# The last store of a row sum, issued by two engines in two halves of the partitions

## The chip, the cores and the metric

The kernel runs on one core of a Trainium2 chip. A core has several engines with queues of their own; three matter here. VectorE (DVE) reduces and adds, ScalarE (ACT) applies a function and can sum what it reads, and SyncE (SP) issues transfers. ScalarE can issue transfers as well. All transfers, whoever issues them, are moved by 16 DMA engines. The metric is the time of one execution on the device in microseconds; lower is better.

## The reference

The input x has 32 x 512 x 1024 values in 32-bit floating point, 67 MB. The output is the sum of each row of 1024 values, so 16,384 sums, 64 KB.

```python
def reference(x):
    return np.sum(x, axis=-1).astype(np.float32)
```

## The kernel before

The 16,384 rows are laid over 128 partitions, so each partition has J = 128 rows. They come in blocks of 16 rows for each partition (BIG), 8 blocks in all. The first 16 x 128 rows of x are one region (x_a, out_a in the code) and the others a second (x_b, out_b, with TWO = 112 rows for each partition). Within a region a partition's rows, and so its sums in the output, lie side by side. The sums are gathered in one tile, sums, of 128 partitions by 128 columns; column j is row j of each partition.

SP issues all loads, in the order in which they are written (helper load, line 93). The first load brings 7 rows of the last block; then come the seven whole blocks, through three buffers, each load waiting until VectorE has summed the block whose buffer it takes. The other 9 rows of the last block come at the end in smaller loads: six rows, two rows, and the last row in two pieces of 536 and 488 values ("left" and "right").

VectorE sums the whole blocks with one instruction each (helper vec, line 100). The rows of the last block are shared out: helper halves (line 109) lets VectorE sum one row by adding its two halves, helper act (line 129) lets ScalarE sum one row. The last row is VectorE's: the left piece first, and then the right piece together with the left one's sum. Semaphores count what is done: acts for ScalarE's rows (10 of them), paired for VectorE's share of each piece (4 with the last row).

The output leaves in three stores. When ScalarE has 7 of its rows done and VectorE the first piece, and the two-row load has landed, ScalarE issues two early stores (lines 185 and 186): columns 16 to 111 to out_b, then columns 0 to 15 to out_a. It then waits for both to land (line 187, semaphore early). SP issues the last store (line 199), of the 16 columns of the last block, after it has waited for all four counts of paired and all of acts (lines 197 and 198), and then waits until it has landed (line 200, semaphore stored). Each of the three stores covers 128 partitions; the last writes 64 bytes for each partition, 8 KB together. Nothing comes after it in the program.

The order on each engine is as written; no planner moves instructions.

Of the kernel before, what the change touches and what calls it, by code (L numbers as in the profile page):

```python
# [30 lines left out]
def kernel(  # L31
# [5 lines left out]
    nc = tc.nc  # L37
# [8 lines left out]
    P = 128  # L46
    batch, seq, dim = x.shape
    rows = batch * seq
    J = rows // P
    BIG = 16  # L50
# [3 lines left out]
    TWO = J - ONE  # L54

    def region(first, n):
        lo, hi = first * P, (first + n) * P
        return (
            x_r[lo:hi, :].rearrange("(p j) d -> p j d", j=n),
            out_r[lo:hi].rearrange("(p j) -> p j", j=n),  # L60
        )

    x_a, out_a = region(0, ONE)
    x_b, out_b = region(ONE, TWO)
# [15 lines left out]
    sums = ctx.enter_context(nc.sbuf_tensor("sums", [P, J], fp32))  # L80
# [4 lines left out]
    def semaphore(name):  # L85
        return ctx.enter_context(nc.semaphore(name=name))

    def block_of(t, a, n):
        return t[:, a * dim : (a + n) * dim].rearrange("p (n d) -> p n d", d=dim)
# [17 lines left out]
    def halves(dst, src):  # L107
        n = src.shape[-1] // 2
        return nc.vector.tensor_tensor_reduce(  # L109
            out=src[:, :n],  # L110
            in0=src[:, :n],
            in1=src[:, n:],
            scale=1.0,
            scalar=0.0,
            op0=mybir.AluOpType.add,
            op1=mybir.AluOpType.add,
            accum_out=dst,
        )

    acts = semaphore("acts")  # L120
    n_acts = 0
# [34 lines left out]
    for landed, j, block in loads[:-1]:  # L156
# [11 lines left out]
    paired = semaphore("paired")  # L168
    pieces = (loads[-1] + (7,), (six, tail + FIRST, block_of(t, FIRST, 6), 2),
              (two, tail + FIRST + 6, block_of(t, FIRST + 6, 2), 1))  # L170
# [10 lines left out]
    early = semaphore("early")  # L181
# [2 lines left out]
    nc.scalar.wait_ge(two, 16)  # L184
    nc.scalar.dma_start(out=out_b[:, : TWO - BIG], in_=sums[:, ONE : J - BIG]).then_inc(early, 16)
    nc.scalar.dma_start(out=out_a, in_=sums[:, :ONE]).then_inc(early, 16)
    nc.scalar.wait_ge(early, 32)

    carried = semaphore("carried")
    nc.vector.wait_ge(left, 16)  # L190
# [2 lines left out]
    nc.vector.wait_ge(carried, 1)  # L193
    halves(sums[:, j : j + 1], whole).then_inc(paired, 1)

    stored = semaphore("stored")
    nc.sync.wait_ge(paired, len(pieces) + 1)
    nc.sync.wait_ge(acts, n_acts)
    nc.sync.dma_start(out=out_b[:, TWO - BIG :], in_=sums[:, J - BIG :]).then_inc(stored, 16)
    nc.sync.wait_ge(stored, 16)  # L200


# [28 lines left out]
```

## Time and profile before

| what | value |
|---|---|
| time, median of 3 runs | 160.7 us (160.56 to 160.77) |
| time of the profiled execution | 160.59 us |
| its span | 159.3 us |
| VectorE busy | 120.7 us, 76% |
| ScalarE busy | 11.9 us, 7% |
| HBM traffic over the span | 422 GB/s |
| chain that ended last | DMA 71%, DVE 27%, SP's queue 1% |

The span is what the hardware profiler records from the first to the last instruction; the time of the execution has 1.3 us more around it. Lines named L199 and the like are lines of the kernel file. A record of a DMA instruction (DMA_DIRECT2D) on SPq or ACTq is the time in which the engine's queue issues the transfer; the transfer itself comes after it and is seen in the busy share of the DMA engines. Waits on semaphores do not count as busy, and have a view of their own.

### The profile page before, as it was taken

How to read it: one execution, taken by the hardware profiler on the slowest of the kernel's cores; microseconds unless marked ns; L12 is line 12 of the kernel's file. 1: busy time of each engine (PE TensorE's matmuls, PEld its weight loads, DVE VectorE, ACT ScalarE, POOL GpSimd, SP SyncE). 2: the span in 40 equal slices, each digit the busy share in tenths (PEclk: the TensorE clock that was granted, in tenths of full speed). 3: DMA queues.
4: the chain of work that ended last, by engine and by line, in shares of the span. 5: the costliest groups of instructions: out<-in, count | busy, mean ns of one | idle time of the engine just before them, and what ended most of it. 6: DMA issues, size and time to landing. Idle time of an engine off the chain costs nothing.

```text
span 159.3 us, 122 instructions
## 1 busy us (share of the span) xinstructions
DVE 120.7 (76%) x40; ACT 11.9 (7%) x21; POOL 0.2 (0%) x4
## 2 busy tenths in 40 slices
DVE  0029600499985999779996899949999499994955
ACT  3000000000000000000000000000000000002993
POOL 0000000000000000000000000000000000000000
DMA  9899799699699699699698996996996996994984
GB/s 331 360 494 527 329 461 527 263 527 527 263 527 527 263 527 527 263 527 510 280 527 346 444 527 263 527 527 263 527 527 263 527 527 263 527 510 214 494 363 148
DMA packets 2160, 67.18 MB, mean 422 GB/s; under 512 B 624, under 2 KB 752, under 8 KB 880
## 3 DMA queue, kind: packets, MB, share of 16 engines
q1 hardware_dynamic: 1872, 67.12, 98.0%
q10 hardware_dynamic: 288, 0.06, 0.2%
HBM read 67.11 MB, written 0.07 MB: 422 GB/s over the span
## 4 chain that ended last, share of the span: by engine, by line
DMA 71%; DVE 27%; SPq 1%; issue 0%
DMA rows<-in_x_dram 71%; DVE sums L100 26%; SPq L93 1%; DVE rows L109 0%; DVE sums L109 0%
## 5 line engine op out<-in xcount | busy, mean ns | idle before, releaser
L100 DVE TENSOR_REDUCE sums<-rows 128x16 f32<-128x16384 f32 (+1 forms) x7 | 110.9, 15848 | 31.6 <-DMA rows<-in_x_dram 31.6
L129 ACT ACTIVATE unread<-rows 128x1024 f32<-128x1024 f32 x10 | 10.1, 1012 | 143.8 <-DMA rows<-in_x_dram 143.8
L109 DVE CUSTOM_DVE_ANT_0 rows<-rows 128x512 f32<-128x512 f32 (+2 forms) x16 | 9.6, 656 | 4.0 <-DMA rows<-in_x_dram 4.0
L129 ACT ACTIVATION_READ_ACCUMULATOR unread<-rows 128x1 f32 x10 | 1.9, 187 | 0.0
L129 ACT ACT_TABLE_LOAD x1 | 1.3, 1283 | 1.4 <-PEq L43 1.4
L109 DVE DVE_READ_ACCUMULATOR2_ANT sums<- 128x1 f32 x15 | 1.2, 83 | 0.0
L155 DVE MEMSET rows<- 128x1 f32 x1 | 0.1, 59 | 1.5 <-PEq L43 1.5
L215 POOL MEMSET const-bfloat16-1.0<- 128x1 bf16 x1 | 0.1, 102 | 0.0
L215 POOL MEMSET const-uint8-127<- 128x1 uint8 x1 | 0.1, 101 | 0.0
L215 POOL MEMSET const-float32-0.0<- 128x1 f32 x1 | 0.1, 99 | 0.2 <-issue 0.2
L215 POOL MEMSET const-float32-1.0<- 128x1 f32 x1 | 0.1, 98 | 0.0
L109 DVE DVE_READ_ACCUMULATOR2_ANT rows<- 128x1 f32 x1 | 0.1, 81 | 0.0
## 6 DMA issues: line engine op xcount, KB each, us to landing
rows<-in_x_dram SPq DMA_DIRECT2D x1, 3584.0 KB, 10.8
rows<-in_x_dram SPq DMA_DIRECT2D x1, 3072.0 KB, 28.7
rows<-in_x_dram SPq DMA_DIRECT2D x1, 1024.0 KB, 30.9
rows<-in_x_dram SPq DMA_DIRECT2D x1, 268.0 KB, 31.1
rows<-in_x_dram SPq DMA_DIRECT2D x1, 244.0 KB, 31.3
rows<-in_x_dram SPq DMA_DIRECT2D x7, 40.8
out_dram<-sums ACTq DMA_DIRECT2D x1, 48.0 KB, 1.6
out_dram<-sums ACTq DMA_DIRECT2D x1, 8.0 KB, 1.6
```

The source lines that it names most:

```text
L93: nc.sync.dma_start(out=dst, in_=src).then_inc(sem, 16)
L100: return nc.vector.tensor_reduce(out=sums[:, j : j + n], in_=block, axis=mybir.AxisListType.X, op=mybir.AluOpType.add,)
L109: return nc.vector.tensor_tensor_reduce(out=src[:, :n], in0=src[:, :n], in1=src[:, n:], scale=1.0, scalar=0.0, op0=mybir.AluOpType.add, op ...
L129: nc.scalar.activation(out=unread[n_acts % len(unread)][:, :], in_=src, func=mybir.ActivationFunctionType.Copy, accum_out=sums[:, j : j + ...
L155: nc.vector.memset(whole[:, width + 1 :], 0.0)
L215: nc = _bacc.Bacc("TRN2", target_bir_lowering=False, num_devices=1)
```

## The change

The last store is cut in two by partitions. SP stores the sums of partitions 0 to 63 and ScalarE those of partitions 64 to 127, 4 KB each. Both engines wait for the same counts of paired and acts first, and both stores count on the semaphore stored, so that SP's last wait is for 32 in place of 16. ScalarE's wait for its two early stores moves from directly behind them to behind its half of the last store.

```diff
     nc.scalar.dma_start(out=out_b[:, : TWO - BIG], in_=sums[:, ONE : J - BIG]).then_inc(early, 16)
     nc.scalar.dma_start(out=out_a, in_=sums[:, :ONE]).then_inc(early, 16)
-    nc.scalar.wait_ge(early, 32)
...
     stored = semaphore("stored")
-    nc.sync.wait_ge(paired, len(pieces) + 1)
-    nc.sync.wait_ge(acts, n_acts)
-    nc.sync.dma_start(out=out_b[:, TWO - BIG :], in_=sums[:, J - BIG :]).then_inc(stored, 16)
-    nc.sync.wait_ge(stored, 16)
+    half = P // 2
+    for engine, lo in ((nc.sync, 0), (nc.scalar, half)):
+        engine.wait_ge(paired, len(pieces) + 1)
+        engine.wait_ge(acts, n_acts)
+        engine.dma_start(
+            out=out_b[lo : lo + half, TWO - BIG :], in_=sums[lo : lo + half, J - BIG :]
+        ).then_inc(stored, 16)
+    nc.scalar.wait_ge(early, 32)
+    nc.sync.wait_ge(stored, 32)
```

## The prediction

> **What bounds the kernel now.** I read the chain of work that ended last first. 71% of it is the transfer of x, 26% VectorE's long reductions, and its last pieces are the row pieces in the closing microseconds. So the 67 MB of loads set the time until 157.35 us, and only what follows the last load can be touched by an edit of the last store. Next come the instructions in order of time from 156 us to the end.
>
> ```profile
> 156.13 0.37 ACTq L185 DMA_DIRECT2D out_dram<-sums  x1
> 156.53 0.56 ACTq L186 DMA_DIRECT2D out_dram<-sums  x1
> ...
> 157.01 0.19 ACT L129 ACTIVATION_READ_ACCUMULATOR unread<-rows 128x1 f32 x1
> ...
> 157.38 0.42 DVE L109 CUSTOM_DVE_ANT_0 rows<-rows 128x245 f32<-128x245 f32 x1 [0.17 <-DMA rows<-in_x_dram]
> 157.72 0.08 DVE L109 DVE_READ_ACCUMULATOR2_ANT sums<- 128x1 f32 x1
> 157.83 0.35 SPq L199 DMA_DIRECT2D out_dram<-sums  x1
> ```
>
> The reader sees start and duration. VectorE writes the last sum at 157.72 + 0.08 = 157.80; SP begins to issue the last store at 157.83 and is through with the issue at 158.18. ScalarE ended its last sum at 157.20 and its two early stores were issued by 157.09, so in the old kernel ScalarE's queue stands idle when the last sum is ready. What the issue costs in nanoseconds is in the answer on the output tensor, and what SP waits for after it in the waits of SP's queue (microseconds in all, times, longest):
>
> ```profile
> L185 ACTq DMA_DIRECT2D out_dram<-sums x1: 374/374/374, 156.1 to 156.1; - x1
> L186 ACTq DMA_DIRECT2D out_dram<-sums x1: 560/560/560, 156.5 to 156.5; - x1
> L199 SPq DMA_DIRECT2D out_dram<-sums x1: 348/348/348, 157.8 to 157.8; - x1
> ...
> SPq L200 <- DMA out_dram<-sums: 1.1, 1, 1.1
> ```
>
> 157.83 + 0.35 + 1.1 = 159.28, the end of the span (159.3). So the last store is 1.45 us on the path, 0.35 in the issue and 1.1 behind it. Where those 1.1 go is shown by stretches of 0.1 us; the last two columns are the busy share of the 16 DMA engines and GB/s:
>
> ```profile
> 157.50:157.60 0.10, 0.10 (x1) 0.00 (x0) 0.00 (x0) 1.00 0.01 1
> 157.60:157.70 0.10, 0.10 (x1) 0.00 (x0) 0.00 (x0) 1.00 0.47 53
> 157.70:157.80 0.10, 0.10 (x2) 0.00 (x0) 0.00 (x0) 1.00 0.27 29
> ...
> 158.50:158.60 0.10, 0.00 (x0) 0.00 (x0) 0.00 (x0) 1.00 0.00 0
> 158.60:158.70 0.10, 0.00 (x0) 0.00 (x0) 0.00 (x0) 1.00 0.12 13
> 158.70:158.80 0.10, 0.00 (x0) 0.00 (x0) 0.00 (x0) 1.00 0.62 55
> 158.80:158.90 0.10, 0.00 (x0) 0.00 (x0) 0.00 (x0) 1.00 0.18 14
> 158.90:159.00 0.10, 0.00 (x0) 0.00 (x0) 0.00 (x0) 1.00 0.00 0
> ```
>
> The packets of the last store move between about 158.65 and 158.9. They begin 0.5 us after the issue ended (158.18), and the span ends 0.4 us behind them. The packets of L186 (issue over at 156.535 + 0.560 = 157.09) begin in the stretch from 157.6: again 0.5 us after the issue's end. So for a small store the path is issue, 0.5 us, packets of some 0.2 us, 0.4 us. What counts for the end is when the later of the two issues is over.
>
> **The change part by part.** *The early wait moves.* ScalarE's wait for its two early stores goes from ahead of the last store to behind ScalarE's half of it. By the DMA issues of the page these stores land 1.6 us after issue, at 157.7 and 158.1, so as the wait stood, it would have kept ScalarE from the new issue until 158.1; moved, it costs nothing: by the time it is reached (after 158.2) both have landed. Nothing else on ScalarE is behind it.
>
> *Two waits are added on ScalarE* (paired, acts), and behind them stands only the new issue. The sum of ScalarE's own is done at 157.20, so paired, at 157.80, decides, as on SP. SP started 0.03 us after it. I take the same for ScalarE; if the wait stands in an instruction of its own, up to 0.08 us (DVE's and ACT's pieces start at 156.04 on the landing of the same load, L185 behind its waits at 156.13). Bounds 0 to +0.08; I take 0, as the idle sequencer is nearest to SP's case.
>
> *SP's store halves to 64 rows.* Its issue is 0.348 us now. SP's other issues, all of 128 rows, take 0.327 to 0.442 us whether a row is 1,952 bytes or 64 KB, so bytes don't set it; whether the number of rows does, no row here shows. Bounds: 0.174 (all by rows) to 0.348 (not at all); I take 0.348, because the rows with very different bytes agree so closely. This half is not what ends last anyhow unless ScalarE's is faster.
>
> *ScalarE's issue is new* and starts at the same 157.83. Nearest rows: an issue of ScalarE with nothing ahead of it, 0.374 (L185), and one of the same 64-byte rows close behind another, 0.560 (L186). SP's own show the same pattern: 0.328 alone, and 0.425 to 0.442 when 0.04 us behind another. So an issue that meets another still under way was 0.10 to 0.19 us longer, on one queue; no two queues issue at once in this trace. Bounds: 0.187 (half of 0.374, all by rows) up to a full turn behind SP's, 0.348 + 0.04 + 0.560 = 0.95 us after 157.83. I take 0.560, because its size, queue and the company of another issue are nearest. It is then over at 158.39 in place of 158.18: +0.21 us.
>
> *Packets.* The three stretches from 158.6 are busy by 0.12 + 0.62 + 0.18 = 0.92 of 0.1 us, so 0.09 us of work on each DMA engine for all rows. Half the rows in the later store save 0.05 us at most; bounds 0 to -0.05, and I take -0.05, since the SP half would be through before ScalarE's begins.
>
> *The wait at the end* counts 32 in place of 16. SP is idle there and the later half decides. The 0.4 us from the last packet to the end are kept; the program around the span (160.59 - 159.3 = 1.3 us) is kept.
>
> Sum against the profiled execution: 160.59 + 0.21 - 0.05 = 160.75 us. This execution is 0.11 below the median of 160.7, so the forecast against the median is 160.86, +0.1%. That is within the 0.2% (0.32 us) that a measurement of this kernel can about tell from no change.
>
> The Trainium skill speaks against the change in DMA: Bandwidth & Descriptors, section Rules for kernel authors: of two transfers to disjoint partition halves it says "Don't bother — they serialize", as both run on the same 16 DMA engines. The stretches above agree with one point only: one store keeps the engines busy 0.09 us of its 1.45, so sharing them costs at most that; by the rule the packets save nothing, and the sum would be 160.91.
>
> **The rivals.** *One issue after the other (slower).* If issues of SP and ScalarE can't run side by side, ScalarE's starts when SP's is over, at 158.18 + 0.04, and takes 0.374 to 0.560: over at 158.59 to 158.78, 0.41 to 0.60 later than the one issue before. Less 0.05 of packets: 161.06 to 161.25. It decides from the point where the joint issue takes more than 0.37 us longer than SP's alone (0.32 + 0.05). For it: issues close behind one another on one queue come every 0.48 us (SP, 0.44 + 0.04) and 0.59 (ScalarE), longer than one alone, so something holds them back. Against it: that something may be the queue's own sequencer, of which there are now two, and a half may hold it for less time.
> The Trainium skill has such a mechanism: Perfetto Trace Analysis, section DMA Instruction — HWDGE, draws a generator of descriptors shared by sequencers, which is locked for exclusive use, with the wait for the lock inside the issue's record. No issue here overlaps one from another queue, so the trace can't confirm it; the longer rows close behind another issue don't contradict it.
>
> *The issues don't meet.* ScalarE's takes its 0.374, or +0.03 on SP's, and the packets save 0.05: 160.68, no change. For it: 0.348 and 0.374 are nearly the same on both queues. Against: every issue close behind another is longer.
>
> *The rows set the issue (faster).* If half the rows halve the issue, each ends 0.17 us earlier; with 0.05 of packets that is 160.48, and if the 0.5 us to the first packet halve too, 160.23. For it: the rows number 128 in every issue here, so nothing excludes it. Against: bytes per row from 64 to 65,536 left the issue within 0.33 to 0.44.
>
> **How the numbers follow.** Forecast, partly meeting issues, 0.40 (own range 160.75 to 161.0, from 0.10 to 0.3 us of meeting). One after the other 0.32. Not meeting 0.18. Rows set it 0.10, of which half is over the 0.2%. Slower by over 0.2% (above 161.02): the serial rival and some of the forecast's upper edge, 0.36. Faster (below 160.38): half of the last rival and a little for the scatter of the three runs (160.56 to 160.77), 0.07. The rest, 0.57, is within. The range for 8 in 10 runs from the upper one of the last rival's two times, 160.48, to the serial rival's upper bound, 161.25; what lies outside is half of the last rival and the scatter at the top.
>
> **What would show it.** In the changed kernel the two issues should both start near 157.83 (shifted with the loads). Right: ScalarE's or SP's issue has a duration of 0.45 to 0.6, its packets begin 0.5 us after its end, and SP's last wait grows by about 0.16. The serial rival: one of the two records is about 0.7 us or longer, or two separate bursts of packets 0.4 us apart. The independent case: both near 0.35 to 0.37 and one burst. The rows: both near 0.2. The forecast is wrong too if ScalarE starts its issue late, or if the 0.4 us behind the packets grow with two stores under way.

## The result, and the profile after

The changed kernel takes 161.27 us (median of 7 runs, 161.21 to 161.37) against 160.75 (7 runs, 160.56 to 161.04). The ratio is 1.0032, with a 95% interval of 1.0022 to 1.0041: slower by 0.52 us. The forecast was 160.86, so its sign was right and its size far too small, and the range missed the time by 0.02 us at its upper end.

The instructions of the changed kernel in order of time (start, duration) and the answer on its output tensor (nanoseconds of an issue) show the first surprise:

```profile
157.79 0.08 DVE L109 DVE_READ_ACCUMULATOR2_ANT sums<- 128x1 f32 x1
157.90 0.53 SPq L201 DMA_DIRECT2D out_dram<-sums  x1
157.90 0.55 ACTq L201 DMA_DIRECT2D out_dram<-sums  x1
...
L201 SPq DMA_DIRECT2D out_dram<-sums x1: 525/525/525, 157.9 to 157.9; - x1
L201 ACTq DMA_DIRECT2D out_dram<-sums x1: 547/547/547, 157.9 to 157.9; - x1
```

Both queues start at the same moment, and both issues are long. SP's, with half the rows, takes 0.525 us where the whole store took 0.348. The waits of SP's queue and the stretches of 0.1 us (busy share of the DMA engines and GB/s in the last two columns) show the second:

```profile
SPq L205 <- DMA out_dram<-sums: 1.4, 1, 1.4
...
159.00:159.10 0.10, 0.00 (x0) 0.00 (x0) 0.00 (x0) 1.00 0.13 14
159.10:159.20 0.10, 0.00 (x0) 0.00 (x0) 0.00 (x0) 1.00 0.26 23
159.20:159.30 0.10, 0.00 (x0) 0.00 (x0) 0.00 (x0) 1.00 0.06 5
159.30:159.40 0.10, 0.00 (x0) 0.00 (x0) 0.00 (x0) 1.00 0.19 18
159.40:159.50 0.10, 0.00 (x0) 0.00 (x0) 0.00 (x0) 1.00 0.23 21
159.50:159.60 0.10, 0.00 (x0) 0.00 (x0) 0.00 (x0) 1.00 0.03 2
```

There are two bursts of packets, 0.3 us apart, each with half the work (0.13 + 0.26 + 0.06 = 0.45 of 0.1 us, and as much again). The first comes 1.17 us after its issue began, by the trace's records of the single packets; before, the whole store's came after 0.84. The second ends at about 159.53, and the span 0.4 us behind it, at 159.9. So the last store's path is now 159.9 - 157.90 = 2.0 us, where it was 1.45: +0.55. The profiled execution of the changed kernel is longer by more than that (161.23 against 160.59), because its last sum was written 0.07 us later (157.79 against 157.72). That is scatter of the loads: in the runs below the same sum stands anywhere from 157.7 to 158.5.

Two causes were open: something about a store of 64 rows, and something about two stores at once.

### The profile page after: what moved, and what is told of

The parts are those of the page before. It is cut to its first block, busy times and chain, and to the rows that moved or that the text cites. A ratio compares the mean times of both kernels' runs of the same rounds, so it can differ in the third digit from the quotient of the medians.

```text
span 159.9 us, 124 instructions
## 1 busy us (share of the span) xinstructions
DVE 120.7 (75%) x40; ACT 11.9 (7%) x21; POOL 0.2 (0%) x4
## 4 chain that ended last, share of the span: by engine, by line
DMA 71%; DVE 27%; SPq 1%; issue 0%
DMA rows<-in_x_dram 71%; DVE sums L100 26%; SPq L93 1%; DVE rows L109 0%; DVE sums L109 0%
```

## The experiments

"Above before" is the difference of medians against runs of the kernel before on the same chip; a bracket is the 95% interval of the ratio. The number of an issue is the duration of its record, one record in one profiled execution of each kernel.

### First set: one queue, one half, ScalarE's queue, two full-height stores

**Both halves from SP** (edit to the changed kernel):

```diff
-    for engine, lo in ((nc.sync, 0), (nc.scalar, half)):
+    for engine, lo in ((nc.sync, 0), (nc.sync, half)):
```

> Both halves of the last store are issued by SP, one close behind the other; ScalarE issues none of it. Theory 1 (what costs is two stores under way together, whichever queue issues them: their transfers are made ready one after the other): the second issue starts 0.04 us behind the first and takes about 0.44, its packets follow about 0.3 us behind the first store's, and the time is 0.4 to 0.6 us above the kernel before. Theory 2 (two queues issuing in the same moment disturb each other, one queue would not): the first issue is 0.35, the lag to its packets 0.5, and the time is at most 0.3 us above before, so clearly less than the changed kernel's 0.52. Theory 3 (ScalarE's queue is slow): less than 0.2 us above before.

Measured: 161.64, 0.91 above before [1.0044, 1.0069]. On one queue the loss is larger than on two, so theories 2 and 3 fall. Theory 1 has the sign but not the size: it took the second issue for 0.44 us and its packets for 0.3 us behind the first store's; they were 0.53, and 0.64 behind. The answer on the output tensor has

```profile
L201 SPq DMA_DIRECT2D out_dram<-sums x2: 526/529/532, 157.9 to 158.5; - x2
```

Even the first, with nothing close ahead of it and nothing from ScalarE beside it, takes 0.53.

**Half a store, alone** (edit to the kernel before):

```diff
-    nc.sync.dma_start(out=out_b[:, TWO - BIG :], in_=sums[:, J - BIG :]).then_inc(stored, 16)
+    half = P // 2
+    nc.sync.dma_start(out=out_b[:half, TWO - BIG :], in_=sums[:half, J - BIG :]).then_inc(stored, 16)
```

> SP alone stores the sums of partitions 0 to 63; those of partitions 64 to 127 of the last 16 columns are left out, so half of the last store is missing from the output. It prices 64 rows against 128 in one store. If the issue, the 0.5 us and the packets go by rows, the time falls by 0.2 us or more and the issue takes near 0.2. If nearly all is fixed for each store, the issue stays at 0.33 to 0.35 and the time falls by 0.05 us or less (0.1 at most).

Measured: 160.99, 0.26 above before [1.0008, 1.0025]. Neither theory expected that less work would be slower. The output tensor's answer and the stretches of this run:

```profile
L200 SPq DMA_DIRECT2D out_dram<-sums x1: 523/523/523, 157.9 to 157.9; - x1
...
159.00:159.10 0.10, 0.00 (x0) 0.00 (x0) 0.00 (x0) 1.00 0.12 13
159.10:159.20 0.10, 0.00 (x0) 0.00 (x0) 0.00 (x0) 1.00 0.28 24
159.20:159.30 0.10, 0.00 (x0) 0.00 (x0) 0.00 (x0) 1.00 0.05 4
```

This is the first burst of the changed kernel at the same place. So half of the loss is there without any second store: 64 rows take 0.17 us longer to issue, and their packets come 0.65 us behind the end of the issue (157.90 + 0.52 = 158.42) and not 0.50, by the records of the single packets.

**The whole store from ScalarE** (edit to the changed kernel):

```diff
-    half = P // 2
-    for engine, lo in ((nc.sync, 0), (nc.scalar, half)):
+    half = P
+    for engine, lo in ((nc.scalar, 0),):
...
-    nc.sync.wait_ge(stored, 32)
+    nc.sync.wait_ge(stored, 16)
```

> ScalarE issues the whole last store of 128 rows, SP none; SP still waits for it at the end. Theories 1 and 2 (two stores together cost): as fast as before within 0.1 us, the issue 0.37, the packets 0.5 us behind its end. Theory 3 (ScalarE's queue is slow): 0.4 to 0.5 us slower than before.

Measured: 160.72, 0.01 below before [0.9991, 1.0009], and the issue:

```profile
L201 ACTq DMA_DIRECT2D out_dram<-sums x1: 338/338/338, 157.9 to 157.9; - x1
```

ScalarE's queue is as good as SP's, and the added waits and the moved early wait, which this kernel has too, cost nothing. Theory 3 falls.

**Two stores of 128 rows at the same moment, cut by columns** (edit to the changed kernel):

```diff
-    half = P // 2
+    half = BIG // 2
...
-            out=out_b[lo : lo + half, TWO - BIG :], in_=sums[lo : lo + half, J - BIG :]
+            out=out_b[:, TWO - BIG + lo : TWO - BIG + lo + half], in_=sums[:, J - BIG + lo : J - BIG + lo + half]
```

> The last store is cut by columns: SP stores 8 columns and ScalarE 8, each for all 128 partitions, both at the same moment. The rows of each store are double those of the changed kernel, at half the bytes. If what the two share goes by rows, the gap between the two bursts of packets grows from 0.29 to near 0.5 us, and the time is 0.8 us or more above before. If it is fixed for each store, the gap stays near 0.3 and the time is 0.5 to 0.65 above before.

Measured: 160.97, 0.24 above before [1.0006, 1.0024], less than either side expected, with twice the rows of the changed kernel. The output tensor's answer and the stretches:

```profile
L201 SPq DMA_DIRECT2D out_dram<-sums x1: 343/343/343, 158.2 to 158.2; - x1
L201 ACTq DMA_DIRECT2D out_dram<-sums x1: 373/373/373, 158.2 to 158.2; - x1
...
159.00:159.10 0.10, 0.00 (x0) 0.00 (x0) 0.00 (x0) 1.00 0.55 31
159.10:159.20 0.10, 0.00 (x0) 0.00 (x0) 0.00 (x0) 1.00 0.89 46
159.20:159.30 0.10, 0.00 (x0) 0.00 (x0) 0.00 (x0) 1.00 0.14 6
```

SP's issue is as short as alone, ScalarE's at most 0.04 us longer than that of its whole store alone (0.373 against 0.338), and the packets of both form one burst. So neither issue waits here for the other to end. Yet there is a loss, and it lies behind the packets: they end before 159.3 and the span at 159.8, 0.5 us later where it was 0.4 before. The row bytes, 32 for each store, also show that it is not the 4 KB of a half that makes the issue long: this store has 4 KB too.

### Second set: the same two stores apart in time, and other row counts

**Two stores of 128 rows, apart** (edit to the kernel before; ScalarE's 8 columns wait only for their own sums):

```diff
-    nc.scalar.wait_ge(early, 32)
...
     stored = semaphore("stored")
+    nc.scalar.wait_ge(paired, len(pieces))
+    nc.scalar.wait_ge(acts, n_acts)
+    nc.scalar.dma_start(out=out_b[:, TWO - BIG : TWO - 8], in_=sums[:, J - BIG : J - 8]).then_inc(stored, 16)
+    nc.scalar.wait_ge(early, 32)
...
-    nc.sync.dma_start(out=out_b[:, TWO - BIG :], in_=sums[:, J - BIG :]).then_inc(stored, 16)
-    nc.sync.wait_ge(stored, 16)
+    nc.sync.dma_start(out=out_b[:, TWO - 8 :], in_=sums[:, J - 8 :]).then_inc(stored, 16)
+    nc.sync.wait_ge(stored, 32)
```

> The last store is cut by columns as in the run before it, two stores of 128 rows on two queues, but not at the same moment: ScalarE's 8 columns leave when its last sum is done, at about 157.25, SP's 8 columns at 157.83 as before. Theory 1 (stores cost only where they are under way together or are of 64 rows): SP's issue 0.35, packets 0.5 us behind its end, the time within 0.1 us of before. Theory 2 (each further store that the last wait counts costs, whenever it was issued): 0.2 us or more above before, as with the cut by columns at the same moment (0.24).

Measured: 160.79, 0.11 above before, not told from it [0.9997, 1.0015]. SP's last issue and wait are those of the kernel before:

```profile
158.03 0.35 SPq L202 DMA_DIRECT2D out_dram<-sums  x1
...
SPq L203 <- DMA out_dram<-sums: 1.1, 1, 1.1
```

A second store does not cost by being counted; it costs when it is issued at the same moment. Here ScalarE's was issued 0.55 us before SP's, and its packets were over before SP's began. That is theory 1, though the median lies just beyond its limit.

**96, 32 and 112 rows, alone.** Each is the half-store kernel with another number:

```diff
-    half = P // 2
+    half = 96
```

(and 32, and 112).

> SP alone stores the sums of partitions 0 to 95; those of 96 to 127 of the last 16 columns are left out of the output. Asked: why does a store of 64 rows take 0.52 us to issue and the one of 128 rows 0.35. Theory A (128 rows are a case of their own, every other count goes a slower way): issue 0.5 to 0.55, first packets 1.1 to 1.2 us after the issue began, 0.2 to 0.35 us above before. Theory B (the fewer rows, the longer, in proportion): issue near 0.43, 0.13 us above before.

> SP alone stores the sums of partitions 0 to 31; those of 32 to 127 of the last 16 columns are left out of the output. Theory A (every count but 128 goes a slower way): issue 0.5 to 0.55 as with 64 rows, the time 0.2 to 0.3 us above before, perhaps a few hundredths less than with 64 rows, as there are fewer packets. Theory B (the fewer rows, the longer): issue near 0.61, 0.4 us above before.

> SP alone stores the sums of partitions 0 to 111; those of 112 to 127 of the last 16 columns are left out of the output. Theory A (every count but 128 goes a slower way): issue 0.5 to 0.55, 0.2 to 0.35 us above before. Theory B (the fewer rows, the longer): issue near 0.39, less than 0.1 us above before.

Measured: 160.71 (0.03 above before), 160.65 (0.03 below) and 160.74 (0.06 above); no interval excludes 1. The issues, in this order:

```profile
L200 SPq DMA_DIRECT2D out_dram<-sums x1: 362/362/362, 157.9 to 157.9; - x1
```

```profile
L200 SPq DMA_DIRECT2D out_dram<-sums x1: 361/361/361, 158.0 to 158.0; - x1
```

```profile
L200 SPq DMA_DIRECT2D out_dram<-sums x1: 358/358/358, 158.1 to 158.1; - x1
```

Both theories fall. 128 is no case of its own, and fewer rows are not slower. The number of rows hardly matters, 32 or 128, and what stands out is 64.

### Third set: what is special about 64

**64 rows of 32 bytes; 64 rows from partition 32; 60 rows; all on SP alone.** Edits to the half-store kernel:

```diff
-    nc.sync.dma_start(out=out_b[:half, TWO - BIG :], in_=sums[:half, J - BIG :]).then_inc(stored, 16)
+    nc.sync.dma_start(out=out_b[:half, TWO - 8 :], in_=sums[:half, J - 8 :]).then_inc(stored, 16)
```

```diff
-    nc.sync.dma_start(out=out_b[:half, TWO - BIG :], in_=sums[:half, J - BIG :]).then_inc(stored, 16)
+    nc.sync.dma_start(out=out_b[32 : 32 + half, TWO - BIG :], in_=sums[32 : 32 + half, J - BIG :]).then_inc(stored, 16)
```

```diff
-    half = P // 2
+    half = 60
```

> SP alone stores 8 columns (32 bytes a row) of partitions 0 to 63; the other 8 of the last 16 columns, and partitions 64 to 127 of all 16, are left out of the output. Asked: why 64 rows of 64 bytes take 0.52 us to issue, when 32, 96, 112 and 128 rows take 0.35 to 0.36. Theory P (the count of 64 partitions is the cause): issue 0.5 to 0.55, first packets near 1.15 us after its start, 0.2 to 0.3 us above before. Theory Q (64 rows of 64 bytes, the square shape, is the cause): issue 0.34 to 0.37, the time within 0.1 us of before.

> SP alone stores partitions 32 to 95, 64 rows from another first partition; the other 64 of the last 16 columns are left out of the output. Theory P (the count of 64): issue 0.5 to 0.55 and 0.2 to 0.3 us above before, as with partitions 0 to 63. Theory R (64 partitions are slow only where they fill one half of the 128): issue 0.35 to 0.37 and within 0.1 us of before.

> SP alone stores partitions 0 to 59; those of 60 to 127 of the last 16 columns are left out of the output. Theory P (64 is a case of its own): issue 0.34 to 0.38, within 0.1 us of before. Theory S (four rows for each DMA engine are the cause; 60 rows can be 15 engines with four each, where 32, 96, 112 and 128 are 16 engines with two, six, seven and eight): issue 0.5 or more, 0.2 to 0.3 us above before.

Measured: 161.12, 0.38 above before [1.0014, 1.0035]; 161.18, 0.44 above [1.0016, 1.0035]; and 160.68, 0.06 below [0.9989, 1.0007]. The issues, in this order:

```profile
L200 SPq DMA_DIRECT2D out_dram<-sums x1: 528/528/528, 157.9 to 157.9; - x1
```

```profile
L200 SPq DMA_DIRECT2D out_dram<-sums x1: 604/604/604, 158.0 to 158.0; - x1
```

```profile
L200 SPq DMA_DIRECT2D out_dram<-sums x1: 409/409/409, 158.0 to 158.0; - x1
```

Theories Q, R and S fall: 64 rows are slow with 32 bytes as with 64, from partition 32 as from 0 (there even 0.08 us longer to issue), and 60 rows are not slow in the end, though their issue is 0.05 above the others (not followed up). The trace bears out what theory S supposes of 60 rows, which makes it a fair test: 15 small packets of 4 bytes go with their 60 packets, where every other store here has 16. So 60 rows come as four for each of these (60 / 15), like 64 (64 / 16), and still their first packet comes 0.84 us behind the start of the issue, as with the whole store; with 64 rows it is 1.17 to 1.24. The two slow ones lost more than the 0.2 to 0.3 expected, by some 0.1 us. In their traces the path from the start of the issue to the last confirmation is 0.28 and 0.35 us longer than before.

**The cut at 96 and 32, two queues at the same moment** (edit to the changed kernel):

```diff
-    half = P // 2
-    for engine, lo in ((nc.sync, 0), (nc.scalar, half)):
+    for engine, lo, half in ((nc.sync, 0, 96), (nc.scalar, 96, 32)):
```

> The changed kernel with another cut: SP stores partitions 0 to 95, ScalarE 96 to 127, at the same moment on two queues. If the change lost its time to the count of 64, this has no such loss: both issues 0.35 to 0.38, the two bursts of packets nearly on top of each other, 0.1 to 0.25 us above before (two stores of 128 rows at once: 0.24). If two partial stores that meet are slow by themselves, the time is as in the changed kernel, about 0.5 above before, with the issues near 0.53 or the bursts 0.3 apart.

Measured: 160.95, 0.21 above before [1.0007, 1.0024]. Output tensor, waits and stretches:

```profile
L200 SPq DMA_DIRECT2D out_dram<-sums x1: 358/358/358, 157.9 to 157.9; - x1
L200 ACTq DMA_DIRECT2D out_dram<-sums x1: 381/381/381, 157.9 to 157.9; - x1
...
SPq L204 <- DMA out_dram<-sums: 1.2, 1, 1.2
...
158.70:158.80 0.10, 0.00 (x0) 0.00 (x0) 0.00 (x0) 1.00 0.26 24
158.80:158.90 0.10, 0.00 (x0) 0.00 (x0) 0.00 (x0) 1.00 0.61 49
158.90:159.00 0.10, 0.00 (x0) 0.00 (x0) 0.00 (x0) 1.00 0.14 9
```

With the line drawn elsewhere, more than half of the change's loss is gone. The issues are short, the packets one burst and as early as those of the kernel before (0.85 us behind the issue's start). What is left is again behind the packets: they end at about 158.97, and the span at 159.5.

### Fourth set: ScalarE's half alone, and a cut near the middle

**ScalarE's half alone** (edit to the changed kernel) and **80 and 48 rows** (edit to the cut at 96 and 32):

```diff
-    for engine, lo in ((nc.sync, 0), (nc.scalar, half)):
+    for engine, lo in ((nc.scalar, half),):
...
-    nc.sync.wait_ge(stored, 32)
+    nc.sync.wait_ge(stored, 16)
```

```diff
-    for engine, lo, half in ((nc.sync, 0, 96), (nc.scalar, 96, 32)):
+    for engine, lo, half in ((nc.sync, 0, 80), (nc.scalar, 80, 48)):
```

> ScalarE alone stores its half, partitions 64 to 127; SP issues none of the last store, so the sums of partitions 0 to 63 of the last 16 columns are left out of the output. Theory P (64 rows are slow on any queue; the rest of the change's loss is the meeting of two such stores): issue 0.5 to 0.55, 0.2 to 0.3 us above before, so that about 0.25 of the change's 0.52 is left for the meeting. Theory V (ScalarE's half alone brings the whole loss, the meeting nothing): about 0.5 us above before.

> The changed kernel with one more cut: SP stores partitions 0 to 79, ScalarE 80 to 127, at the same moment. Theory P (of the counts only 64 is slow): both issues 0.35 to 0.39 and 0.15 to 0.25 us above before, as with 96 and 32. Theory W (counts near one half are slow as well): an issue of 0.45 or more, 0.35 us or more above before.

Measured: 160.99, 0.31 above before [1.0011, 1.0029], and 160.85, 0.17 above [1.0001, 1.0018]. The issues of the one, then of the other:

```profile
L201 ACTq DMA_DIRECT2D out_dram<-sums x1: 522/522/522, 157.9 to 157.9; - x1
```

```profile
L200 SPq DMA_DIRECT2D out_dram<-sums x1: 357/357/357, 157.8 to 157.8; - x1
L200 ACTq DMA_DIRECT2D out_dram<-sums x1: 382/382/382, 157.9 to 157.9; - x1
```

Theory P holds twice, though 0.31 is just above its range and leaves 0.21 for the meeting. 64 rows are slow on either queue, and 80 and 48 are not. ScalarE's 0.547 in the changed kernel is so nearly the 0.522 that it takes with nothing beside it that the meeting adds at most 0.025 to the issue.

### Fifth set: is it the shared semaphore?

The same two cuts, at 96 and at 64, with a semaphore for each store:

```diff
     stored = semaphore("stored")
+    stored_act = semaphore("stored_act")
...
-        ).then_inc(stored, 16)
+        ).then_inc(stored if engine is nc.sync else stored_act, 16)
...
-    nc.sync.wait_ge(stored, 32)
+    nc.sync.wait_ge(stored_act, 16)
+    nc.sync.wait_ge(stored, 16)
```

> The cut into 96 and 32 partitions on two queues again, but each store has a semaphore of its own, and SP waits for 16 on each of the two in place of 32 on one. With one semaphore this cut cost 0.21 us, though issues and packets were nearly as early as before; the time behind the last packet was 0.5 us in place of 0.4. Theory X (32 increments of one semaphore arrive one after the other): the time behind the last packet is 0.4 again, and the kernel is within 0.1 us of before. Theory Y (the stores' ends are delayed by having two of them under way): 0.15 to 0.25 us above before, as with one semaphore.

> The changed kernel, 64 and 64 partitions, with a semaphore for each store. There the two bursts of packets are 0.3 us apart, so the increments of the two stores don't meet. Theories X and Y both: no gain, 0.45 to 0.55 us above before. A gain of 0.15 us or more would mean that the shared semaphore is a part of what the change lost.

Measured: 160.90, 0.18 above before [1.0002, 1.002], and 161.23, 0.51 above [1.0017, 1.0039]. So sharing the semaphore costs nothing that can be seen; theory X falls in the form in which it was put, and the first time lies in theory Y's range. What remains can be read from the trace's records of the single increments, by which a store's landing is confirmed (16 for each store). In the kernel before, the 16 increments of the last store arrive from 159.085 to 159.255, one about every 11 ns. In the cut at 96 with two semaphores, SP's 16 arrive from 159.310 to 159.473 and ScalarE's 16 from 159.484 to 159.639, although the packets of both stores ran together and were over by 159.135. With one semaphore the 32 arrive from 159.148 to 159.477 in the same way. So the confirmations of two stores come one after the other, whichever semaphore they go to, and 16 more of them take 0.16 us, which is the 0.17 to 0.24 us that the cuts without 64 rows lost. Why they queue is not shown. With 64 and 64 rows the second burst begins 0.28 us behind the first, with one semaphore as with two, so the semaphore doesn't part the bursts either.

## Why the prediction was wrong

**Where the path is.** Right. Everything up to the last sum is as before but for 0.07 us of scatter, and the whole change is in the 1.45 us of the last store's path, now 2.0.

**The moved wait and the added waits.** Right at zero: ScalarE's issue starts at 157.90 like SP's, and the whole store from ScalarE is as fast as before.

**SP's half, 0.348, bounds 0.174 to 0.348.** This is the first step that failed, though the half that ends last is ScalarE's. It measured 0.525, outside the bounds. The argument was that rows of very different bytes agree closely, so the shape doesn't set the issue. But all those rows had 128 partitions; nothing in the trace spoke of another count, and no upper bound above the whole store's price was kept, since half a store was taken to cost at most a whole one. The half alone cost 0.26 us more than the whole. The rival "the rows set the issue" had the wrong sign for 64 and nothing to act on for 32, 96 and 112.

**ScalarE's issue, 0.560.** The number is nearly right (0.547) by luck. It was taken from issues close behind another on one queue, as the price of two issues that meet. But two issues on two queues at the same moment take 0.358 and 0.381, or 0.343 and 0.373, nearly as if alone (0.362, 0.348, and 0.338 from ScalarE). It is the 64 rows that take 0.522 alone. So the sign that the prediction named for itself, an issue of 0.45 to 0.6, appeared for another cause. Nor is the row that it rests on, L186, a fixed price: in the traces of these runs the same store's issue takes 0.455 to 0.575.
The Trainium skill, Perfetto Trace Analysis, section DMA Instruction — HWDGE, puts a wait for a locked generator of descriptors into the issue's record. For issues without 64 rows the records leave room for at most 0.04 us of such a wait; whether 64 rows hold something for long isn't told apart by the runs.

**0.5 us from the issue's end to the packets.** This is the step that made the size. It was carried over as fixed. By the records of the single packets it measured 0.65 for SP's half (issue over at 158.43, packets from the stretch at 159.0) and 0.90 for ScalarE's (158.45, packets from 159.3). Alone, half a store has 0.65 as well, from either queue, so 0.15 belongs to 64 rows, and the other 0.25 comes when a second such store is issued at the same moment. With both halves on SP's queue, the second issued 0.62 us behind the first, each has its packets 0.65 behind its issue's end. Of the cuts tried, only that into two 64-row stores parts the bursts: with 96 and 32, 80 and 48, or 128 and 128, they run together. What the second burst waits for is not shown.

**Packets, -0.05.** Each burst has half the work, as worked out, but as it starts later, nothing is gained.

**0.4 us behind the packets.** Nearly right for the changed kernel (159.53 to 159.9), where the bursts are apart. For stores that run together it grows to 0.5, which the prediction named as a way to be wrong.

The prediction's own sum with what the trace has for ScalarE's half: +0.20 for the issue (+0.21 forecast), +0.40 for the time to the packets (nothing forecast), -0.03 for the packets and -0.03 behind them, together the +0.55 of the path. By runs: half a store alone costs 0.26 (0.31 from ScalarE), and the rest of the 0.52, 0.21 to 0.26, comes with the second store, whose burst is 0.28 behind the first. The serial rival, at 161.06 to 161.25, came within 0.02 of the time, and its sign of two separate bursts is there, 0.28 apart and not 0.4. Its mechanism, one issue over before the other starts, is not: both records are about equally long and start together. That its number is close is chance.

The Trainium skill's sentence that two transfers to disjoint halves of the partitions are not worth it (DMA: Bandwidth & Descriptors, section Rules for kernel authors) has the right outcome. Its reason, the DMA engines in common, explains at most 0.05 us of the 0.52 here: together the two bursts keep the engines busy for 0.09 us, as the one store did, so one half has at most the 0.045 of the other to wait for.

No version tried that stores everything beats the kernel before. One store of 128 rows, from either queue, is the best of them, and only the two stores apart in time were not told from it.

## What to carry to other kernels

A small store's time on the path is nearly all fixed (here 1.45 us for 128 rows and less than 0.1 less for 32), so cutting it in two can save only hundredths of a microsecond, and here a second store issued at the same moment cost 0.17 to 0.24 us even without 64 rows. When a shape changes, do not bound its price by rows that all have the old shape: half of the work may cost more than the whole, and one run with the new shape alone tells it. Where two stores were issued at once at the end, it helped here to avoid the count of 64 partitions.

## What was unexpected of the hardware

- A store of exactly 64 partitions takes 0.52 to 0.60 us to issue, from SP or ScalarE, from partition 0, 32 or 64, with 32 or 64 bytes a row; last stores of 32, 48, 80, 96, 112 and 128 partitions take 0.34 to 0.38, and of 60, 0.41. Alone at the end of the kernel it costs 0.26 to 0.44 us by the medians, 0.27 to 0.35 on the traces' path. Why is open; loads, longer rows and counts between 60 and 80 other than 64 were not tried.
- Two 64-row stores issued at the same moment have their packets 0.28 us apart, in both traces of such a pair; of the other pairs tried (96 and 32, 80 and 48, 128 and 128) the packets run together. Why is open.
- Two issues from two queues at the same moment took 0.36 and 0.38 us (96 and 32 rows), nearly as alone; two 64-row stores from one queue come one after the other (1.16 us for both), and that kernel lost 0.91 us against the 0.52 of two queues.
- The increments of two stores that run together arrive one after the other, 10 to 11 ns apart, 32 in 0.33 us, on one semaphore or on two.
